# Own buffers for the token fetch, norm rows spread on TensorE, residual rows loaded earlier

## The chip, the cores and the metric

One core of a Trainium2 chip runs the whole program. The core has TensorE (matrix products and transposes), VectorE, ScalarE, GpSimd and the sync engine, which in this kernel only issues DMAs; 16 DMA engines move data between HBM and SBUF, the on-chip memory of 128 partitions. The metric is the time of one execution on the device in microseconds (us); lower is better.

## What is computed

One encoder layer: an attention mixer with a norm, then a mixture of experts with a second norm. Only the second part is touched. `x` has 512 tokens of 1024 channels.

```python
x = layer_norm(ALPHA * x + mixed, ln1_g, ln1_b)          # called h below
g_probs = softmax(x @ w_group + b_group)                 # best of 4 groups, then the best 2 of its 8 experts
combine = one_hot(group) * g_val * expert_w              # weight of each of 32 experts for each token
for g in range(4):                                       # 8 experts in each group, d_expert = 256
    hid = silu(einsum('nd,edf->nef', x, w_gate[g])) * einsum('nd,edf->nef', x, w_up[g])
    y = y + einsum('nef,efd->nd', hid * combine[:, g, :, None], w_down[g])
out = layer_norm(ALPHA * x + y, ln2_g, ln2_b)
```

## The kernel before

The attention part fills about the first 410 us and is left as it is. Then the experts follow, 0 to 31, in `trunk`'s last loop (lines 1278 to 1300). Tokens are gathered: each expert has 64 places, two experts make a pair, so a pair has a table column of 128 token numbers, `toki`, which `finish_routing` writes (line 920).

For expert `e` the loop calls `gate_up(e)` (16 matmul records in the trace, named sc<-we), `down(e - 1)` (8 records, tr<-we) and `act(e)` (four small transposes stp, then Silu). Every expert reads six weight tiles `we` of 128 x 1024 floats (0.5 MB each): four for gate and up, two for down; 192 in all. They are loaded by the sync queue in the order of use (`raw_load`, line 1018), up to `AHEAD` = 44 ahead of their use. The tiles' places are given by `RING` (line 67): a cycle of 40 entries, in which 0 is the pool `slots` (20 buffers), 1 is `slots2` (15 buffers), 2 and 3 are the pools `hip` and `lop` (4 each). The last 40 loads all go to `slots`. A load can be issued only when the tile that had its place has been used.

The first two pairs take their tokens from SBUF through products with one-hot matrices (`prep_first`). From pair 2 on, `fetch(p)` (line 1063) lets GpSimd gather 128 rows of h from HBM (`hD`) with an indirect DMA into a tile xg; there are `XGB` = 3 of these, taken from `slots2` when first needed and cleared by GpSimd. `prep_x` (line 1075) transposes such a tile on TensorE in two halves of four transposes each (pj<-ident,xg) and copies them to a tile xp. After the second expert of a pair, GpSimd scatters the pair's output rows oe to `y2D` in HBM (line 1147; oe has two buffers). The last two pairs, experts 28 to 31, stay in SBUF as tiles `late`.

Behind `act(28)` stand `gain_rows` (line 1181), which loads the two rows of the last norm (gain and bias) to one partition over ScalarE's DMA queue and spreads each over 128 partitions by two products with a row of ones, and `last_rows` (line 1157), which loads h again as four tiles hb and then y2D as eight tiles yy, both over the sync queue.

`finish` (line 1219) works off the list `FIN` step by step: `sum` adds two yy tiles on GpSimd, `open` begins the PSUM sum fin of one half of 128 tokens with hb times the identity, `add` adds the late rows by one-hot products, `rows` adds the yy sums, then the norm's statistics (`stat`, `root`, `gain`, `end`) and the stores follow.

Each engine works its own queue in order. Tile's scheduler sets the order of the instructions in the experts' part, and so may bring forward what is written later. The hardware-issued DMAs of the sync queue and of ScalarE share eight completion semaphores, named DMAHW0 to DMAHW7 below and handed out in turn; a DMA waits until the one before it on the same semaphore has landed.

Of the kernel before, what the change touches and what calls it, by code (L numbers as in the profile page):

```python
# [9 lines left out]
F32 = mybir.dt.float32  # L10
# [8 lines left out]
P = 128  # L19
S = 512  # L20
D = 1024
# [22 lines left out]
XEB = 4  # L44
AHEAD = 44
EARLY = 13
# [14 lines left out]
}  # L61
XGB = 3
H_POOL = (0, 1, 2, 3)
LATE_C = (2, 3)
H_STT = (0, 1, 2, 3)

RING = [0] * 8 + [1] * K2 + [0] * 12 + [2] * 4 + [3] * 4 + [1] * (NSLOT2 - XGB - K2)
SCB = 2
# [9 lines left out]
FIN_TAG = ("pj", "pj", "tr", "sc", "sc", "av", "tr", "tr")  # L78
FIN_AT = {}
FIN = (  # L80
# [17 lines left out]
def trunk(ctx, tc, xT, x, wm, wv, wbr, wout, wr, br, bg, rbx, lnp, lncol, wexp, out):  # L98
# [24 lines left out]
    def mm(ps, a, b, start, stop):  # L123
        pin(nc.tensor.matmul(ps, a, b, start=start, stop=stop))  # L124
# [23 lines left out]
    bgs = const.tile([P, 16], F32, name="bgs")  # L148
    lnc = const.tile([P, 2, C], F32, name="lnc")
    nc.gpsimd.dma_start(lnc, lncol)  # L150
# [4 lines left out]
    def slot(shape, dtype, name, pool=None):  # L155
        return (pool or slots).tile(shape, dtype, tag="slot", name=name)
# [535 lines left out]
    tok2 = keep.tile([P, 2 * NLATE], F32, name="tok2")  # L692
    flag = keep.tile([P, 1], I32, name="flag")
    onehot = keep.tile([P, TT, 4 * CAP], F32R, name="onehot")
    nc.gpsimd.memset(ones, 1.0)
# [364 lines left out]

    xg = []

    def fetch(p):
        if len(xg) < XGB:
            xg.append(slot([P, D], F32, f"xg{p}", slots2))
            nc.gpsimd.memset(xg[-1], 0.0)
        nc.gpsimd.indirect_dma_start(
            out=xg[(p - 2) % XGB], out_offset=None, in_=hD[:, :],
            in_offset=bass.IndirectOffsetOnAxis(ap=toki[:, p : p + 1], axis=0),
            bounds_check=S - 1, oob_is_err=False,  # L1070
        )
# [85 lines left out]
    def last_rows():  # L1157
# [12 lines left out]
        for tt in range(TT):  # L1170
            hb.append(slot([P, D], F32, f"hb{tt}", slots2))
            nc.sync.dma_start(hb[tt], hD[tt * P : (tt + 1) * P, :])
        for tt in range(TT):
            y2.append([slot([P, D], F32, f"yy{tt}{k}") for k in range(2)])
            for k in range(2):
                nc.sync.dma_start(y2[tt][k], y2v[tt, k])

    ones1 = bp.tile([1, P], F32, name="ones1")
    nc.gpsimd.memset(ones1, 1.0)

    def gain_rows():

        for k in range(2):
            gb2.append(lop.tile([P, D], F32, tag="lo", name=f"gb2{k}"))
            nc.scalar.dma_start(gb2[k][0:1, :], lnp[2 + k].unsqueeze(0))
            for j in range(2):
                ps = pb.tile([P, S], F32, tag="pj", name="pj", bufs=NBUF["pj"])
                mm(ps, ones1, gb2[k][0:1, j * S : j * S + S], True, True)
                nc.scalar.activation(gb2[k][:, j * S : j * S + S], ps, AF.Copy)
# [88 lines left out]
    for e in range(NE):  # L1278
# [12 lines left out]
        if 2 <= e < NE - 2:  # L1291
            prep_x(e // 2 + 1, e % 2)
            if e % 2 and e // 2 + 1 + XGB < NPAIR:
                fetch(e // 2 + 1 + XGB)
        if e == NE - 4:
            gain_rows()
            last_rows()
# [65 lines left out]
def layout(inputs):  # L1363
# [29 lines left out]
    lnp = np.stack([a["ln1_g"][0], a["ln1_b"][0], a["ln2_g"][0], a["ln2_b"][0]])  # L1393
    lncol = lnp[:2].reshape(2, C, P).transpose(2, 0, 1)
    gu = np.concatenate([a["w_gate"][0].reshape(NE, D, 256), a["w_up"][0].reshape(NE, D, 256)], 2)
# [23 lines left out]
```

## Time and profile before

| | us |
|---|---|
| median of 3 runs | 701.72 (699.74 to 704.83) |
| the profiled execution's own time | 704.91 |
| its span, first to last instruction | 703.2 |
| TensorE busy in the span | 651.9 (93%) |
| VectorE, ScalarE, GpSimd busy | 394.8, 322.8, 87.2 |
| moved by DMA | 160.15 MB, mean 228 GB/s |

A share of the span says little here: the attention part and the experts have different limits. So the stretch from 410 us on is read by itself: windows for who is busy, waits for who stands still, and the timeline for the order of events. A matmul's record is modelled and overlaps with the next one, so the pace is read from starts, not from the length of one record.

### The profile page before, as it was taken

The numbers are of one execution on the slowest core, as the hardware profiler recorded it, in microseconds if no ns is written. First come the engines' busy times: TensorE is split into PE (matmuls) and PEld (weight loads), VectorE is DVE, ScalarE is ACT, GpSimd is POOL, SyncE is SP. The second block draws the span as 40 slices with busy tenths as digits, with TensorE's granted clock in tenths as the row PEclk, the third lists the DMA queues.
The fourth block names the chain that finished last, engine by engine and source line by source line (L and its number), as shares of the span: only waits on it lengthen the run. The fifth ranks groups of instructions, "written<-read, shape, count | busy, mean of one in ns | idle before, by whom it ended". The sixth has DMA issues, their size and how long they took to land.

```text
span 703.2 us, 8791 instructions
## 1 busy us (share of the span) xinstructions
PE 651.9 (93%) x3072; PEld 425.1 (60%) x3072; DVE 394.8 (56%) x818; ACT 322.8 (46%) x632; POOL 87.2 (12%) x135
## 2 busy tenths in 40 slices
PE   8999998999999999999999979389999989999893
PEld 4888786888878878888888763133333333223251
DVE  5786868767777886464937973113323232322337
ACT  5777777866755666654422323112322222322312
POOL 2010100111000000040001330401111120100043
PEclk9999999999999999999999979889999999989997
DMA  9500095102130322138946689969999999499943
GB/s 335 234 1 1 1 348 220 62 6 86 46 105 23 113 76 89 61 114 301 334 192 223 226 334 409 410 248 412 408 409 411 406 404 404 161 365 410 410 191 122
DMA packets 48323, 160.15 MB, mean 228 GB/s; under 512 B 7440, under 2 KB 7584, under 8 KB 48276
## 3 DMA queue, kind: packets, MB, share of 16 engines
q1 hardware_dynamic: 44208, 152.26, 57.1%
q0 software_dynamic: 4064, 7.30, 2.8%
q8 instruction: 25, 0.41, 0.2%
q14 instruction: 22, 0.18, 0.1%
q10 hardware_dynamic: 4, 0.01, 0.0%
HBM read 151.20 MB, written 15.73 MB: 237 GB/s over the span
## 4 chain that ended last, share of the span: by engine, by line
PE 60%; issue 14%; DVE 12%; DMA 8%; ACT 3%; POOL 2%; SPq 0%; POOLq 0%; DVEq 0%
PE pj L124 23%; PE sc L124 9%; PE pv L124 6%; PE pb L124 6%; PE po L124 4%; DMA we<-in_wexp_dram 3%; PE tr L124 3%; PE av L124 2%; PE fin L124 2%; DMA xg<-hD,toki 2%; PE tr L521 2%; DMA hb<-hD 1%; DVE hp L804 1%; DVE gus L1106 1%; DMA y2D<-oe,rowi 1%
## 5 line engine op out<-in xcount | busy, mean ns | idle before, releaser
L124 PE MATMUL sc<-we,xp 128*64 128x512 f32 x448 | 117.6, 609 | 0.0
L124 PE MATMUL pj<-xh,wh 128*128 128x512 f32 x256 | 102.5, 402 | 2.6 <-DVE k L335 1.6
L124 PE MATMUL pj<-xh,wl 128*128 128x512 f32 x256 | 101.0, 394 | 0.5 <-DVE wl L109 0.5
L124 PE MATMUL pj<-xl,wh 128*128 128x512 f32 x256 | 100.8, 394 | 0.2 <-DVE xl L109 0.2
L124 PE MATMUL tr<-we,sg 128*64 128x512 f32 x256 | 78.6, 608 | 1.6 <-DVE sg L1119 1.6
L109 DVE TENSOR_TENSOR wl<-raw,wh 128x1024 fp32r<-128x1024 f32 (+1 forms) x57 | 68.4, 1205 | 20.4 <-ACT wh L106 20.1
L1106 DVE TENSOR_TENSOR gus<-gus,sc 64x512 f32<-64x512 f32 x32 | 21.7, 679 | 86.4 <-ACT gus L1105 86.3
L124 PEld LDWEIGHTS sc<-we,xp 128*64 128x64 f32 x448 | 33.0, 139 | 57.0 <-issue 53.5
L1105 ACT ACTIVATE gus<-sc 64x512 f32<-64x512 f32 x32 | 19.0, 593 | 105.4 <-PE sc L124 78.2
L106 ACT ACTIVATE wh<-raw 128x1024 fp32r<-128x1024 f32 (+1 forms) x57 | 58.7, 1038 | 16.9 <-PE pj L124 5.2
L124 PEld LDWEIGHTS pj<-xh,wh 128*128 128x128 f32 x256 | 48.4, 189 | 12.9 <-ACT wh L106 2.1
L124 PEld LDWEIGHTS pj<-xh,wl 128*128 128x128 f32 x256 | 48.3, 189 | 12.0 <-DVE wl L109 1.7
L124 PEld LDWEIGHTS pj<-xl,wh 128*128 128x128 f32 x256 | 48.5, 189 | 8.8 <-DVE xl L109 0.5
L124 PE MATMUL pb<-y,wh 128*128 128x512 f32 x128 | 39.9, 393 | 1.9 <-DVE k L335 1.9
L124 PEld LDWEIGHTS tr<-we,sg 128*64 128x64 f32 x256 | 21.1, 137 | 30.2 <-issue 26.6
L109 DVE TENSOR_TENSOR wl<-tr,wh 128x512 fp32r<-128x512 f32 (+1 forms) x64 | 30.8, 485 | 9.9 <-ACT wh L106 9.4
L1082 PE MATMUL pj<-ident,xg 128*128 128x128 f32 x112 | 19.6, 297 | 14.5 <-DMA xg<-hD,toki 14.5
L106 ACT ACTIVATE wh<-tr 128x512 fp32r<-128x512 f32 (+1 forms) x64 | 27.5, 431 | 12.1 <-PE tr L521 11.0
L474 POOL TENSOR_SCALAR_AFFINE_SELECT w<-w 128x128 f32<-128x128 f32 x32 | 14.5, 466 | 147.4 <-ACT w L471 144.7
L1147 POOL DMA_INDIRECT y2D<-oe,rowi x14 | 14.0, 1001 | 141.0 <-DVE oe L1145 141.0
L1082 PEld LDWEIGHTS pj<-ident,xg 128*128 128x128 f32 x112 | 12.5, 146 | 30.9 <-issue 13.7
L124 PE MATMUL sc<-k,q 128*128 128x512 f32 (+3 forms) x128 | 29.2, 324 | 0.9 <-DVE w L470 0.9
(222 smaller groups left out, 1205.4 us busy)
## 6 DMA issues: line engine op xcount, KB each, us to landing
we<-in_wexp_dram SPq DMA_DIRECT2D x192, 512.0 KB, 10.7
raw<-in_wm_dram SPq DMA_DIRECT2D x32, 512.0 KB, 4.9
raw<-in_wv_dram SPq DMA_DIRECT2D x8, 512.0 KB, 8.7
y2D<-zero SPq DMA_DIRECT2D x16, 256.0 KB, 3.9
raw<-in_wbr_dram SPq DMA_DIRECT2D x8, 512.0 KB, 5.5
raw<-in_wout_dram SPq DMA_DIRECT2D x8, 512.0 KB, 4.9
yy<-y2D SPq DMA_DIRECT2D x8, 512.0 KB, 10.2
strip<-in_rbx_dram SPq DMA_DIRECT2D x8, 256.0 KB, 4.2
```

Of the source, the lines that this page charges most:

```text
L106: act = nc.scalar.activation(hi, src, AF.Copy)
L109: pin((eng or nc.vector).tensor_sub(lo, src, hi.bitcast(F32)), fix == "both")
L124: pin(nc.tensor.matmul(ps, a, b, start=start, stop=stop))
L474: nc.gpsimd.affine_select(out=blk, in_=blk, pattern=[[-1, P]], compare_op=OP.is_gt, fill=0.0, base=0, channel_multiplier=1)
L521: nc.tensor.transpose(tr[:, i * P : (i + 1) * P], w[:, off + j * P : off + (j + 1) * P], ident)
L804: nc.vector.scalar_tensor_tensor(out=src, in0=src, scalar=r, in1=lnb[:, cs], op0=OP.mult, op1=OP.add)
L1082: nc.tensor.transpose(ps[:, c, :], xg[(p - 2) % XGB][:, o : o + P], ident)
L1105: nc.scalar.activation(gus[e], ps[CAP:], AF.Copy)
L1106: nc.vector.tensor_add(gus[e], gus[e], ps[:CAP])
L1147: nc.gpsimd.indirect_dma_start(out=y2D[:, :], out_offset=bass.IndirectOffsetOnAxis(ap=rowi[:, p : p + 1], axis=0), in_=oe[p], in_offset=No ...
```

## The change

The three fetch tiles xg get a place of their own (the pool `keep`) and are cleared when the tables for the routing are made. The three places in `slots2` go to weights: the ring has 43 entries, `AHEAD` is 47, and the last 43 loads go to `slots`. The norm's rows are no longer loaded to one partition: `lnc`, which already brought the first norm's rows as columns (channel on the partition), now brings all four, and for each of 16 blocks VectorE copies a column over 128 columns (bc, two buffers) and TensorE multiplies that with the identity. The loads of hb are written at expert 20 instead of 28, and the sums 0 to 3 are opened, and given the late rows that exist, from expert 29 on. The memory for GpSimd's DMA descriptors is set to 2048 bytes of a partition; the line gave no size before.

```diff
-AHEAD = 44
+AHEAD = 47
+HB_AT = 20
-RING = [0] * 8 + [1] * K2 + [0] * 12 + [2] * 4 + [3] * 4 + [1] * (NSLOT2 - XGB - K2)
+RING = [0] * 8 + [1] * K2 + [0] * 12 + [2] * 4 + [3] * 4 + [1] * (NSLOT2 - K2)
-FIN_AT = {}
+FIN_AT = {29: (0, 1, 2, 3)}
 FIN = (
-    "sum0 sum1 sum2 open0 open1 open2 open3 down31 open4 add4.2 add0.3 add1.3 add2.3 add3.3 add4.3 open5 add5.3 open6 add6.3 "
+    "sum0 sum1 sum2 down31 open4 add4.2 add0.3 add1.3 add2.3 add3.3 add4.3 open5 add5.3 open6 add6.3 "
...
-    lnc = const.tile([P, 2, C], F32, name="lnc")
+    lnc = const.tile([P, 4, C], F32, name="lnc")
...
+    xg = [keep.tile([P, D], F32, name=f"xg{k}") for k in range(XGB)]
+    for t in xg:
+        nc.gpsimd.memset(t, 0.0)
...
     def fetch(p):
-        if len(xg) < XGB:
-            xg.append(slot([P, D], F32, f"xg{p}", slots2))
-            nc.gpsimd.memset(xg[-1], 0.0)
...
         for tt in range(TT):
-            hb.append(slot([P, D], F32, f"hb{tt}", slots2))
-            nc.sync.dma_start(hb[tt], hD[tt * P : (tt + 1) * P, :])
-        for tt in range(TT):
             y2.append([slot([P, D], F32, f"yy{tt}{k}") for k in range(2)])
...
-    ones1 = bp.tile([1, P], F32, name="ones1")
-    nc.gpsimd.memset(ones1, 1.0)
...
             gb2.append(lop.tile([P, D], F32, tag="lo", name=f"gb2{k}"))
-            nc.scalar.dma_start(gb2[k][0:1, :], lnp[2 + k].unsqueeze(0))
             for j in range(2):
                 ps = pb.tile([P, S], F32, tag="pj", name="pj", bufs=NBUF["pj"])
-                mm(ps, ones1, gb2[k][0:1, j * S : j * S + S], True, True)
+                for q in range(4):
+                    c = 4 * j + q
+                    bc = bp.tile([P, P], F32, tag="bc", name="bc", bufs=2)
+                    nc.vector.tensor_copy(bc, lnc[:, 2 + k, c : c + 1].to_broadcast([P, P]))
+                    mm(ps[:, q * P : (q + 1) * P], bc, ident, q == 0, q == 3)
                 nc.scalar.activation(gb2[k][:, j * S : j * S + S], ps, AF.Copy)
...
+        if e == HB_AT:
+            for tt in range(TT):
+                hb.append(slot([P, D], F32, f"hb{tt}", slots2))
+                nc.sync.dma_start(hb[tt], hD[tt * P : (tt + 1) * P, :])
...
-    nc = bacc.Bacc("TRN2", target_bir_lowering=False, num_devices=1)
+    nc = bacc.Bacc("TRN2", target_bir_lowering=False, num_devices=1, dynamic_dma_scratch_size=2048)
```

How the instructions stand on the engines, at three places. A row is one instruction of the queue or several alike: its line, the operation, the tile written and the tiles read; the number behind a weight is its place among the 192, and the lines of the changed kernel are shifted.

The start of the fetches, on GpSimd before. y2D<-oe is a pair's scatter, xg2 to xg4 are the tiles for pairs 2 to 4.

```order
L947 TENSOR_TENSOR cw_3016<-cw_3016,small_oe_2972 128x32 x4
L1147 DMA y2D_60<-oe_4183,rowi_3017 1024x1024
L1147 DMA y2D_60<-oe_4287,rowi_3017 1024x1024
L1066 MEMSET xg2_4203 128x1024
L1066 MEMSET xg3_4208 128x1024
L1067 DMA xg2_4203<-hD_61,toki_3018 128x1024
L1067 DMA xg3_4208<-hD_61,toki_3018 128x1024
```

GpSimd at the same place now, where xg0 to xg2 are the tiles for pairs 2 to 4.

```order
L951 TENSOR_TENSOR cw_3016<-cw_3016,small_oe_2972 128x32 x4
L1066 DMA xg0_3024<-hD_61,toki_3018 128x1024
L1066 DMA xg1_3025<-hD_61,toki_3018 128x1024
L1066 DMA xg2_3026<-hD_61,toki_3018 128x1024
L1146 DMA y2D_60<-oe_4193,rowi_3017 1024x1024
L1066 DMA xg0_3024<-hD_61,toki_3018 128x1024
```

The three fetches stood behind the scatters of pairs 0 and 1; now they stand ahead of both.

TensorE before, from the end of gate_up(3) (weight 19) on to expert 3's down product and the first transposes (weights 20 and 21 are expert 2's down product, 26 and 27 expert 3's).

```order
L124 MATMUL sc_4267<-we19_4027,xe0_1_3989 64x512 x2
L124 MATMUL tr_4288<-we20_4029,sg_4257 64x512 x2
L124 MATMUL tr_4288<-we21_4031,sg_4257 64x512 x2
L1113 MATMUL stp_4299<-ident_63,gus_4284 128x64 x4
L124 MATMUL tr_4336<-we26_4041,sg_4304 64x512 x2
L124 MATMUL tr_4336<-we27_4043,sg_4304 64x512 x2
L1082 MATMUL pj_4261<-ident_63,xg2_4203 128x128 x4
L1082 MATMUL pj_4307<-ident_63,xg2_4203 128x128 x4
```

TensorE now, from the end of gate_up(2) on, whose last weight is 13.

```order
L125 MATMUL sc_4222<-we13_4019,xe0_1_3993 64x512 x2
L1081 MATMUL pj_4265<-ident_63,xg0_3024 128x128 x2
L125 MATMUL tr_4242<-we14_4021,sg_4210 64x512 x2
L125 MATMUL tr_4242<-we15_4023,sg_4210 64x512 x2
L1112 MATMUL stp_4256<-ident_63,gus_4239 128x64 x4
L1081 MATMUL pj_4265<-ident_63,xg0_3024 128x128 x2
L125 MATMUL sc_4271<-we16_4025,xe0_0_3980 64x512 x2
```

The first transposes stood behind all of expert 3; now they stand between gate_up(2) and gate_up(3), and expert 3's down product has moved behind gate_up(4)'s start.

The bunch of transposes on TensorE now, at expert 14 (xg0 holds pair 8 and at the end 11, xg1 pair 9, xg2 pair 10).

```order
L125 MATMUL sc_4761<-we79_4395,xp6_4656 64x512 x2
L1081 MATMUL pj_4801<-ident_63,xg2_3026 128x128 x2
L1081 MATMUL pj_4853<-ident_63,xg0_3024 128x128 x4
L125 MATMUL tr_4782<-we80_4419,sg_4751 64x512 x2
L1081 MATMUL pj_4899<-ident_63,xg0_3024 128x128 x2
...
L1081 MATMUL pj_4951<-ident_63,xg1_3025 128x128 x4
L125 MATMUL sc_4810<-we82_4427,xp7_4754 64x512 x2
...
L125 MATMUL sc_4810<-we84_4439,xp7_4754 64x512 x2
L1081 MATMUL pj_5095<-ident_63,xg2_3026 128x128 x4
L1081 MATMUL pj_5147<-ident_63,xg0_3024 128x128 x2
L125 MATMUL sc_4810<-we85_4443,xp7_4754 64x512 x2
```

TensorE before at the same expert: one half per expert, with pair 7's second half at the top and pair 8's first half below.

```order
L1082 MATMUL pj_4797<-ident_63,xg4_4213 128x128 x4
L124 MATMUL sc_4806<-we82_4439,xp7_4750 64x512 x2
L124 MATMUL sc_4806<-we83_4464,xp7_4750 64x512 x2
L124 MATMUL tr_4826<-we86_4476,sg_4794 64x512
L124 MATMUL sc_4806<-we84_4468,xp7_4750 64x512 x2
L124 MATMUL sc_4806<-we85_4472,xp7_4750 64x512 x2
L124 MATMUL tr_4826<-we86_4476,sg_4794 64x512
L124 MATMUL tr_4826<-we87_4485,sg_4794 64x512 x2
L1082 MATMUL pj_4849<-ident_63,xg2_4203 128x128 x4
```

A like bunch stood before at weights 108 to 118, with pairs 10 to 14; it has moved some four experts ahead. The norm rows' 16 products have moved from experts 25 and 26 to experts 21 to 23.

The sync queue before, with the semaphores that each load waits for, from weight 150 on.

```order
L1024 DMA we151_5011<-in_wexp_dram 128x1024 [waits DMAHW1_49,PE_49]
L1024 DMA we152_5015<-in_wexp_dram 128x1024 [waits DMAHW3_49,PE_49]
L1024 DMA we153_5023<-in_wexp_dram 128x1024 [waits DMAHW5_49,PE_49]
L1024 DMA we154_5027<-in_wexp_dram 128x1024 [waits DMAHW6_49,PE_49]
L1024 DMA we155_5052<-in_wexp_dram 128x1024 [waits DMAHW7_49,PE_49]
L1024 DMA we156_5056<-in_wexp_dram 128x1024 [waits DMAHW0_49,PE_49]
L1024 DMA we157_5060<-in_wexp_dram 128x1024 [waits DMAHW1_49,PE_49]
L1024 DMA we158_5064<-in_wexp_dram 128x1024 [waits DMAHW2_49,PE_49]
L1024 DMA we159_5073<-in_wexp_dram 128x1024 [waits DMAHW3_49,PE_49]
L1024 DMA we160_5077<-in_wexp_dram 128x1024 [waits DMAHW4_49,PE_49]
```

The sync queue now, at the new place of hb's loads.

```order
L1028 DMA we168_5125<-in_wexp_dram 128x1024 [waits DMAHW2_49,PE_49]
L1028 DMA we169_5129<-in_wexp_dram 128x1024 [waits DMAHW3_49,PE_49]
L1294 DMA hb0_5153<-hD_61 128x1024 [waits DMAHW4_49]
L1294 DMA hb1_5155<-hD_61 128x1024 [waits DMAHW5_49]
L1294 DMA hb2_5157<-hD_61 128x1024 [waits DMAHW6_49]
L1294 DMA hb3_5159<-hD_61 128x1024 [waits DMAHW7_49]
L1028 DMA we170_5162<-in_wexp_dram 128x1024 [waits DMAHW0_49,PE_49]
L1028 DMA we171_5166<-in_wexp_dram 128x1024 [waits DMAHW1_49,PE_49]
```

Before, the turn skips DMAHW2 ahead of weight 152 and DMAHW4 ahead of 153: ScalarE's two loads have them, so weights 158 and 160 wait for those. Now nothing is skipped, and hb's four loads have moved from behind weight 191 to behind 169; on TensorE the opens of sums 0 and 1 stand behind gate_up(28), those of 3 and 2 inside and behind gate_up(29).

## Rows read from the trace of the kernel before

**Rows 1.** Windows: start:end and length, busy time (instructions) of each engine, clock, DMA.

```profile
449.00:472.00 23.00, 11.63 (x52) 5.06 (x54) 2.23 (x4) 2.07 (x4) 7.82 (x8) 0.78 0.78 288
472.00:600.00 128.00, 123.89 (x596) 47.16 (x594) 38.58 (x66) 33.67 (x65) 18.97 (x19) 1.00 1.02 407
600.00:624.00 24.00, 22.90 (x88) 6.58 (x82) 7.36 (x17) 7.04 (x13) 1.19 (x2) 0.86 0.56 196
```

**Rows 2.** Timeline 426 to 463 us: start, length, engine, line, tiles, count [idle before].

```profile
430.62 0.17 DVE L920 TENSOR_SCALAR toki<-slotp 128x16 int32<-128x16 f32 x1 [0.50 <-PE slotp L124]
...
434.83 1.94 PE L124 MATMUL sc<-we,xe 128*64 128x512 f32 x8
...
446.12 1.94 PE L124 MATMUL tr<-we,sg 128*64 128x512 f32 x8 [1.56 <-DVE sg L1119]
...
450.82 1.86 POOL L1066 MEMSET xg<- 128x1024 f32 x2
452.85 1.04 POOL L1067 DMA_INDIRECT xg<-hD,toki  x1 [0.17 <-DMA we<-in_wexp_dram]
...
456.43 0.99 POOL L1067 DMA_INDIRECT xg<-hD,toki  x1 [0.27 <-POOL xg L1066]
...
460.37 1.97 PE L1082 MATMUL pj<-ident,xg 128*128 128x128 f32 x8 [12.31 <-DMA xg<-hD,toki]
```

**Rows 3.** Waits of the sync queue: us in total, times, longest.

```profile
SPq L1024 <- PE sc L124: 23.1, 23, 13.8
...
SPq L1024 <- DMA gb<-in_lnp_dram: 17.1, 2, 13.2
```

**Rows 4.** Timeline 608 to 634 us, the norm rows' loads and products.

```profile
610.11 1.92 ACTq L1185 DMA_DIRECT2D gb<-in_lnp_dram  x2
...
613.42 1.12 PE L124 MATMUL pj<-gb,ones 1*128 1x512 f32 x2
...
626.19 0.66 PE L1082 MATMUL pj<-ident,xg 128*128 128x128 f32 x4
```

**Rows 5.** The page's first line.

```profile
span 703.2 us, 8791 instructions
```

**Rows 6.** Timeline 660 to 684 us, the end of the experts and the opened sums.

```profile
661.20 1.08 PE L124 MATMUL tr<-we,sg 128*64 128x512 f32 x4
...
664.18 5.40 PE L124 MATMUL fin<-hb,ident 128*128 128x512 f32 x8 [1.90 <-DMA hb<-hD]
...
669.51 1.94 PE L124 MATMUL tr<-we,sg 128*64 128x512 f32 x8
670.73 2.36 POOL L1217 TENSOR_TENSOR yy<-yy,yy 128x1024 f32<-128x1024 f32 x1 [24.62 <-DMA yy<-y2D]
...
671.93 4.01 PE L124 MATMUL fin<-late,stl 128*128 128x512 f32 x15
...
679.35 1.88 PE L124 MATMUL fin<-yy,ident 128*128 128x512 f32 x4
```

**Rows 7.** The tile xg: its 14 fetches, from issue to landing.

```profile
DMA to landing us min/median/max: 4.8/7.4/8.4
```

**Rows 8.** Timeline of GpSimd, 470 to 600 us: three of the scatters, one per pair.

```profile
481.82 1.02 POOL L1147 DMA_INDIRECT y2D<-oe,rowi  x1 [5.88 <-DVE oe L1145]
...
549.82 1.00 POOL L1147 DMA_INDIRECT y2D<-oe,rowi  x1 [5.85 <-DVE oe L1145]
...
585.93 1.02 POOL L1147 DMA_INDIRECT y2D<-oe,rowi  x1 [16.56 <-DVE oe L1145]
```

**Rows 9.** Timeline of TensorE, 596 to 682 us: gate_up of experts 24, 25 and 28.

```profile
603.58 3.60 PE L124 MATMUL sc<-we,xp 128*64 128x512 f32 x16
...
609.89 3.60 PE L124 MATMUL sc<-we,xp 128*64 128x512 f32 x16
...
636.87 3.60 PE L124 MATMUL sc<-we,xp 128*64 128x512 f32 x16
```

**Rows 10.** Timeline of VectorE, 300 to 312 us: copies of a column over 128 columns.

```profile
306.71 0.53 DVE L670 COPY small_xe<-lnc 128x128 f32<-128x128 f32 x2
```

More of the change, by code (lines that the diff above doesn't have):

```diff
@@ L1058, in evac_x @@
             nc.vector.tensor_copy(dst, src)
-    xg = []
     def fetch(p):
-        if len(xg) < XGB:
-            xg.append(slot([P, D], F32, f"xg{p}", slots2))
-            nc.gpsimd.memset(xg[-1], 0.0)
         nc.gpsimd.indirect_dma_start(
@@ L1393, in layout @@
     lnp = np.stack([a["ln1_g"][0], a["ln1_b"][0], a["ln2_g"][0], a["ln2_b"][0]])
-    lncol = lnp[:2].reshape(2, C, P).transpose(2, 0, 1)
+    lncol = lnp.reshape(4, C, P).transpose(2, 0, 1)
     gu = np.concatenate([a["w_gate"][0].reshape(NE, D, 256), a["w_up"][0].reshape(NE, D, 256)], 2)
```

## The prediction

> **What bounds the kernel now.** I read the windows by stage first, because the change touches only what runs after 430 us. From 472 to 600 us the DMA engines move 407 GB/s at a share of 1.02 (full), and TensorE is busy 123.9 of 128 us [rows 1]: expert weights come as fast as they can and TensorE works them off, so a gain needs both. Then I looked for the places where one of the two stands still. There are two, and both are holes in the DMA stream as well.
>
> The first lies at 449 to 472 us: TensorE is busy 11.6 of 23 us, DMA share 0.78 [rows 1]. The timeline says why: the table of token numbers, toki, is ready at 430.8 us, but GpSimd issues the first fetch of token rows at 452.85, and TensorE's first transposes of them stand idle for 12.31 us until it lands [rows 2]. Meanwhile the weight buffers fill up and the sync queue waits 13.8 us in one piece for TensorE to free one [rows 3].
>
> The second is at 600 to 624 us: share 0.56 [rows 1]. TensorE is busy there, at a granted clock of 0.86 in the mean, so part of the time at 1.2 instead of 2.4 GHz; the stream stops because the sync queue's weight loads wait 17.1 us, 13.2 of it in one piece, for the two small loads of the last norm's rows [rows 3], which ScalarE issues only at 610.11 us, when its own queue gets there [rows 4]. The order shows the link: loads 158 and 160 wait for the channels DMAHW2 and DMAHW4 that those two took.
>
> Last I read the end. TensorE finishes expert 30's down product at 662.3 us, waits for hb, opens four sums in 5.40 us, runs down(31) until 671.45, and 31.75 us of sums, statistics and stores follow up to 703.2 [rows 5, 6].
>
> The sums are made against the profiled execution's span of 703.2 us. Its own time is 704.9 us, 3.2 above the median of the three runs (701.7); I take the difference in us over to the median.
>
> **The change, part by part.**
>
> *Fetch buffers of their own.* Nothing of the weight ring must come free, so the order puts the fetches of pairs 2, 3 and 4 ahead of all scatters. The first starts when toki is written, 430.9 us. Landings take 4.8 to 8.4 us, median 7.4 [rows 7]; with the stream full I take 7.4: 438.3 us. TensorE now has the first transposes behind gate_up(2), which ends at about 436.3 (the two records of load 16 taken off the end of the row at 434.83 [rows 2]). It waits 2.0 us (0 to 3.0), with expert 3's work queued behind. Gone are 12.31 us idle, 0.8 us because eight transposes, right behind the idle time and at the lower of the clock's two levels (mean 0.78 over the window [rows 1]), took 1.97 us instead of 2 x 0.6 [rows 2, 4], and 1.56 us ahead of down(3)'s products [rows 2], which now stand inside expert 4's. **Gain 12.31 + 0.8 + 1.56 - 2.0 = 12.6 us** (11.6 to 14.6).
> The three memsets (two take 1.86 us [rows 2], so 2.8 us of GpSimd) move to the end of the attention part, ahead of the index tables at 305 us that VectorE converts. I take 0: projections keep TensorE busy there. Without that cover it is 2.8 us.
>
> The Trainium skill (DMA: Bandwidth & Descriptors, section "Queues, rings and completion order") says that each DMA engine changes round-robin between the queues that have work, packet by packet. By that a fetch would pass the queued weights and land near the shortest of the rows, 4.8 us, before TensorE asks; TensorE's sum would be 2.0 us better. The median row, taken under a full stream, is 7.4 and speaks against it; the sum goes by the row.
>
> *The bunch of transposes.* Both orders pull several pairs' transposes together. Before, it lies at experts 18 and 19: two pairs of experts take 585.93 - 549.82 = 36.1 us where two others take 27.2 (five in 68.0 us) [rows 8]: 8.9 us more, of which eight halves brought forward are 8 x 0.6 = 4.7 [rows 4], paid back later, and some 4 are waits. Now it lies at experts 13 to 15. Pair 10's fetch can go out only behind pair 7's last transposes, and about 6.5 us of TensorE work stands between that and pair 10's transposes; a landing of 7.4 then leaves 1 us, pair 11 another. I take **0**; bounds -4 (no wait) and +12 (two more landings, little covered).
>
> *The norm rows.* Out: two loads and four one-row products. From expert 25 to 28 TensorE needs 636.87 - 609.89 = 26.98 us, against 3 x 6.31 without them [rows 9]: 8.05 us of products (1.1 each), their half clock and one half of transposes (0.6) [rows 4]. In: sixteen products of the transposes' shape at 0.15 each (2.4), around experts 21 to 23. Each waits for a copy on VectorE (two take 0.53 us [rows 10]) with two buffers; expert 22's matmuls stand between them, and behind the copies on VectorE stands that expert's gate sum. For these waits I take 1.5 us (0 to 8, every copy and product in turn). **Gain 8.05 - 0.6 - 2.4 - 1.5 = 3.5 us** (-3 to 5). And no load waits for a ScalarE channel any more.
>
> *hb and the opened sums.* Between down(30) and down(31) lie 7.2 us [rows 6]. About 0.4 remain for expert 31's gate. The four opens move to experts 28 and 29; at the full clock one takes 1.05 (two records, as the 1.1 of a product of that size [rows 4]), 4.2 in all. **Gain 2.6 us** (0 if they run slowly, 6.8 if they fall into waits for weights). Eight products of late rows also move ahead of down(31): 8 x 0.27 = 2.1 us [rows 6], no change in the sum. hb's four loads now run behind load 169, so the last weights come 5.2 us later than they would, and y2's rows are next behind them.
>
> **TensorE's sum:** 12.6 + 3.5 + 2.6 = **18.7 us**; down(31) ends at 671.45 - 18.7 + 2.1 = 654.9.
> **The stream's own limit:** filling the holes gives (1.02 - 0.78)/1.02 x 23 = 5.4 and (1.02 - 0.56)/1.02 x 24 = 10.8 us, 16.2 together [rows 1]. The first two y2 loads landed by 670.7 [rows 6], so now by 654.5; the last weight two loads of 1.29 us earlier (0.52 MB at 407 GB/s), 651.9. down(31) cannot end before 651.9 + 1.94 = 653.8. So TensorE sets the end by about 1 us: the two limits nearly meet, and a larger gain on TensorE alone is worth at most that.
> The tail then is 31.75 - 2.1 = 29.6 us. GpSimd's first sum of y2 ends at 654.5 + 2.4 = 656.9, before TensorE wants it (654.9 + 5.8 = 660.7), so it covers itself. End: 654.9 + 29.6 = 684.5, which is **683.0 us** on the median's scale.
>
> **Rivals.**
> *The first fetch passes the weights (7%).* Landing after 4.8 us, it ends TensorE's new wait; 2.0 us less there, but the stream's limit lets 1.0 through: 682. For it: the shortest landing [rows 7]. Against: the median. It is the skill's rule above.
> *A hole stays (10%).* The change does not do what it says for the stream: the sync queue meets another late thing, hb at load 170 or the last 43 loads, which have only 20 buffers. For it: TensorE ends only 1 us behind the stream, so any delay shows. Against: the holes' causes are gone from the order. With the second hole left, weights end at 662.7, down(31) at 664.6, the kernel at 694.2: 692.7.
> *The wait moves into the bunch (7%).* Two more landings uncovered at experts 13 to 15: +12 us, 695. For it: three buffers, four pairs in one and a half experts. Against: the same pattern cost some 4 us before.
> *GpSimd's transfers come one at a time (3%).* The smaller scratch lets GpSimd issue an indirect transfer only when the one before has landed. At 7.4 us each from 431, pair 9's fetch is the 13th (527 us), pair 10's the 15th (542), pair 11's the 16th (549); TensorE wants them from about 519 on (pair 5's scatter at 481.82 + 3 x 13.6 = 522.6, expert 14 six us later, less 12.6), and waits 8 + 13 + 5 us; pair 6's scatter lands at 579 and holds one of two output buffers, some 3 more. 683 + 29 = 712, slower. It decides between one and two in flight: with two, pair 9 lands by 480. Against: before, fetches started at 452.85 and 456.43 [rows 2], two at least in flight; the small scratch itself is in no trace here. The skill's page (same title, section "Terms") makes a descriptor 16 bytes, so 2048 would be 128 of them per ring; eight rows for each of 16 engines make that, as an estimate from the page, a dozen transfers.
>
> **How the numbers follow.** The forecast has 73%, the quicker first fetch 7, a hole that stays 10, the bunch 7, one at a time 3. Likeliest 683.0. TensorE's best case ends at the stream's limit, 681.9, and the runs of before spread 2.5 us each way; upward the range takes in the stayed hole. **678 to 693** leaves out about the bunch, the slow case and half of what the forecast's worst terms hold. 1% (7 us) is about what a measurement of this kernel tells from no change: faster 0.89, same 0.08, slower 0.03.
>
> **What would show it.** First fetch near 431 us; at most 3 us idle before the first transposes; no wait of weight loads on a ScalarE load; a DMA share of 1.0 from 449 on until the last y2 row; clock 1.0 at experts 25 to 28; down(31) ending near 655. The prediction is wrong if TensorE idles over 6 us in all at experts 13 to 15, if a later queue wait opens the stream again, or if weights land after 655 us although the stream was never idle.

## The result and the profile after

The changed kernel takes **695.33 us** (median of 4 runs, 693.07 to 695.99); the kernel before, run beside it, 702.34. The ratio is **0.9889** (95% interval 0.9862 to 0.9917). A second set of six runs gave 696.45 and 0.9915 (0.9887 to 0.9944). So the change is worth about 7 us of time where 18.7 were forecast, and 695.3 lies outside 678 to 693. The profiled execution's span is 694.3 us (its own time 695.99), 8.9 us under that of before [rows 5].

The windows of the changed kernel, with the columns of [rows 1]:

```profile
449.00:472.00 23.00, 23.00 (x114) 9.15 (x112) 7.51 (x14) 6.58 (x13) 3.79 (x4) 1.00 1.03 409
472.00:600.00 128.00, 121.06 (x590) 46.16 (x584) 41.07 (x84) 33.86 (x64) 17.32 (x18) 1.00 1.03 408
600.00:624.00 24.00, 22.04 (x110) 7.71 (x112) 6.47 (x12) 5.79 (x12) 1.94 (x2) 1.00 0.94 360
624.00:648.00 24.00, 21.85 (x92) 6.93 (x90) 5.91 (x10) 5.34 (x10) 0.98 (x1) 1.00 1.03 411
```

Both holes of the DMA stream are gone: share 1.03 for 0.78 in the first window, 0.94 for 0.56 in the third, and the granted clock is 1.00 at 600 to 624 us where it was 0.86. These are the signs that the prediction named. Yet TensorE gained less than half.

The timeline at the first fetch (start, length, engine, line, operation, tiles, count, idle before), which answers [rows 2]:

```profile
432.03 1.09 POOL L1066 DMA_INDIRECT xg<-hD,toki  x1 [14.50 <-DVE rowi L925]
433.43 1.00 POOL L1066 DMA_INDIRECT xg<-hD,toki  x1 [0.30 <-issue]
434.74 0.99 POOL L1066 DMA_INDIRECT xg<-hD,toki  x1 [0.31 <-issue]
439.51 0.44 PE L1081 MATMUL pj<-ident,xg 128*128 128x128 f32 x2 [1.80 <-DMA xg<-hD,toki]
```

Three fetches are issued within 2.7 us, the first lands after 7.4 us, and TensorE waits 1.80 us for it, not 12.31. That wait is the prediction's almost to the tenth. Behind it comes something that the prediction did not count. These are the products of down(1), and later those of down(2):

```profile
439.88 3.58 PE L125 MATMUL tr<-we,sg 128*64 128x512 f32 x8
...
447.64 1.89 PE L125 MATMUL tr<-we,sg 128*64 128x512 f32 x8
```

The same eight records take 1.7 us longer behind the wait: the granted clock is 0.57 at 440 to 444 us.

Where the rest went is read from one comparison: the start of the same gate_up in both kernels. First the kernel before, experts 9 and 20 (24 and 28 stand in [rows 9] as 603.58 and 636.87):

```profile
494.15 1.07 PE L124 MATMUL sc<-we,xp 128*64 128x512 f32 x2
...
577.60 1.08 PE L124 MATMUL sc<-we,xp 128*64 128x512 f32 x4
```

Then the changed kernel, experts 9, 20, 24 and 28, and the last twelve products of down(30) and down(31):

```profile
483.57 1.07 PE L125 MATMUL sc<-we,xp 128*64 128x512 f32 x2
...
568.25 1.51 PE L125 MATMUL sc<-we,xp 128*64 128x512 f32 x6
...
601.61 1.89 PE L125 MATMUL sc<-we,xp 128*64 128x512 f32 x8
...
626.85 1.46 PE L125 MATMUL sc<-we,xp 128*64 128x512 f32 x6
...
660.99 2.80 PE L125 MATMUL tr<-we,sg 128*64 128x512 f32 x12
```

TensorE's lead over the kernel before is the difference of these starts, and its steps can be set beside those of the prediction:

| up to | lead, us | step | the prediction's step |
|---|---|---|---|
| expert 9 | 10.6 | +10.6, first fetch | +12.6 |
| expert 20 | 9.35 | -1.2, bunch of transposes | 0 |
| expert 24 | 1.97 | -7.4, the norm's rows | -4.5 (2.4 + 1.5 + half 0.6) |
| expert 28 | 10.0 | +8.05, no one-row products | +8.05 |
| end of down(31), 671.45 and 663.8 | 7.7 | -2.4, opens and late rows | +0.5 (2.6 less 2.1 moved ahead) |
| end, 703.2 and 694.3 | 8.9 | +1.2, tail | +2.1 |

No single wait took the gain. Four steps came out smaller than forecast, all on the same side, 8.9 us up to down(31). A second trace of the changed kernel agrees in the two largest: 33.36 us from expert 20 to 24 in both, 36.94 from expert 28 to the end of down(31) for 36.93 here.

The bunch of transposes, with TensorE's waits for fetches and the uncut sixteen records of a gate_up behind it, in the changed kernel:

```profile
524.32 0.63 PE L1081 MATMUL pj<-ident,xg 128*128 128x128 f32 x4 [0.69 <-DMA xg<-hD,toki]
...
528.03 0.41 PE L1081 MATMUL pj<-ident,xg 128*128 128x128 f32 x2 [1.48 <-DMA xg<-hD,toki]
...
532.49 3.60 PE L125 MATMUL sc<-we,xp 128*64 128x512 f32 x16
535.92 1.03 PE L125 MATMUL tr<-we,sg 128*64 128x512 f32 x4
537.60 0.46 PE L1112 MATMUL stp<-ident,gus 64*128 64x64 f32 x4 [0.65 <-DVE gus L1105]
```

And the wait in the bunch of the kernel before:

```profile
570.26 0.41 PE L1082 MATMUL pj<-ident,xg 128*128 128x128 f32 x2 [2.15 <-DMA xg<-hD,toki]
```

The norm's rows, experts 21 to 22, in the changed kernel's timeline:

```profile
581.70 1.29 PE L125 MATMUL pj<-ident,bc 128*128 128x128 f32 x6
582.93 1.08 PE L125 MATMUL sc<-we,xp 128*64 128x512 f32 x4
583.94 0.49 PE L125 MATMUL pj<-ident,bc 128*128 128x128 f32 x2
584.35 1.08 PE L125 MATMUL sc<-we,xp 128*64 128x512 f32 x4
585.36 1.30 PE L125 MATMUL pj<-ident,bc 128*128 128x128 f32 x6
```

and the group of all of them, from the lines of TensorE at 560 to 600 us (records, busy us, mean ns, idle before):

```profile
L125 PE MATMUL pj<-ident,bc 128*128 128x128 f32 x32 | 6.5, 310 | 0.3
```

There are 32 records, not 16: a product of two f32 tiles leaves two records where a transpose leaves one. TensorE hardly idles there (0.3 us); it works. And a group of four gate_up products that is cut off from the next by other products takes 1.01 us from start to start (582.93 to 583.94), against 0.86 in the uncut sixteen above (532.49 to 535.92, 3.43 for four groups). So each cut costs 0.15 us here.

The end of the experts, the counterpart of [rows 6]: expert 31's gate_up with late rows between, and the opens that are left.

```profile
652.35 1.03 PE L125 MATMUL sc<-we,xp 128*64 128x512 f32 x4
654.08 0.73 PE L125 MATMUL fin<-late,stl 128*128 128x512 f32 x2 [0.70 <-DVE late L113]
654.74 1.07 PE L125 MATMUL sc<-we,xp 128*64 128x512 f32 x2
655.75 0.73 PE L125 MATMUL fin<-late,stl 128*128 128x512 f32 x2
```

The same stands in expert 30. TensorE waits 0.70 us each time for VectorE to write the late rows, with the rest of gate_up queued behind.

### The profile page after: what moved, and what is told of

The parts are those of the page before. It is cut to its first block, busy times and chain, and to the rows that moved or that the text cites. A ratio compares the mean times of both kernels' runs of the same rounds, so it can differ in the third digit from the quotient of the medians.

```text
span 694.3 us, 8852 instructions
## 1 busy us (share of the span) xinstructions
PE 652.4 (94%) x3096; PEld 425.1 (61%) x3096; DVE 399.3 (58%) x834; ACT 323.2 (47%) x632; POOL 86.9 (13%) x134
## 4 chain that ended last, share of the span: by engine, by line
PE 59%; DVE 16%; issue 14%; ACT 6%; DMA 3%; POOL 2%; SPq 0%; POOLq 0%; DVEq 0%; ACTq 0%
PE pj L125 19%; PE sc L125 12%; PE pv L125 6%; PE pb L125 6%; PE po L125 4%; PE tr L125 3%; PE av L125 2%; PE fin L125 2%; DVE gus L1105 2%; PE tr L522 1%; DVE wl L110 1%; ACT wh L107 1%; PE stp L1112 1%; DVE hp L808 1%; DMA y2D<-oe,rowi 1%
## 5 line engine op out<-in xcount | busy, mean ns | idle before, releaser
L125 PE MATMUL sc<-we,xp 128*64 128x512 f32 x448 | 115.2, 600 | 0.0
L125 PE MATMUL tr<-we,sg 128*64 128x512 f32 x256 | 76.5, 616 | 0.0
L125 PEld LDWEIGHTS tr<-we,sg 128*64 128x64 f32 x256 | 19.7, 137 | 26.9 <-issue 22.5
L1112 PEld LDWEIGHTS stp<-ident,gus 64*128 64x128 f32 x128 | 10.3, 138 | 36.1 <-DVE gus L1105 28.7
L125 PEld LDWEIGHTS pb<-y,wh 128*128 128x128 f32 x128 | 23.3, 188 | 7.1 <-PE tr L522 1.7
```

The lines of the kernel that those rows point to most:

```text
L1112: nc.tensor.transpose(st[:, q, :], gus[e][:, q * P : (q + 1) * P], ident[:CAP, :CAP])
```

## The experiments

Two theories were set against each other. **W**: TensorE's own work sets the end everywhere, and the terms for that work were too small. **S** (later L, and H for a hole in it): the weight stream sets the end, so that what TensorE gains is lost again where weights are late. Spans of one kernel differ by some 2 us for a reason that no edit here touches: the experts' first matmul starts between 419.2 and 422.5 us over all profiled executions, and the granted clock of 411 to 449 us lies between 0.84 and 0.96. So within a trace I read the distance between two experts, not the absolute time.

### Each part alone

**The fetch buffers alone.** The kernel before with

```diff
-AHEAD = 44
+AHEAD = 47
-RING = [0] * 8 + [1] * K2 + [0] * 12 + [2] * 4 + [3] * 4 + [1] * (NSLOT2 - XGB - K2)
+RING = [0] * 8 + [1] * K2 + [0] * 12 + [2] * 4 + [3] * 4 + [1] * (NSLOT2 - K2)
+    xg = [keep.tile([P, D], F32, name=f"xg{k}") for k in range(XGB)]
...
+    nc = bacc.Bacc("TRN2", target_bir_lowering=False, num_devices=1, dynamic_dma_scratch_size=2048)
```

> The kernel before, with the first part of the change alone: three fetch tiles of their own, their three places given to weights, the small descriptor memory; norm rows and hb as before. Theory W (TensorE's own work sets the end everywhere): in the changed kernel TensorE stood 10.6 us ahead of before at expert 9 and 9.4 us at expert 20, so this part alone is worth 9.4 us and gives a ratio of 0.987 (0.984 to 0.990): more than the whole change measured (0.9889). Theory S (the weight stream sets the end): the hole for the norm's two loads is still there, only 5.4 us of stream are filled; ratio 0.992. First fetch lands near 439 us and TensorE waits 1.8 us for it in both.

Measured: 701.00 us, ratio 0.995 (0.9927 to 0.9973), span 699.6. That is neither: TensorE's lead was 11.6 us at expert 9 and 10.3 at expert 28, as W says, but only 3.6 at the end. Windows of this kernel, its sync queue's wait for the norm's loads, and TensorE's end of the experts:

```profile
520.00:560.00 40.00, 35.62 (x180) 13.20 (x178) 11.51 (x20) 9.79 (x19) 6.68 (x7) 1.00 0.82 314
560.00:600.00 40.00, 37.64 (x154) 11.80 (x150) 12.71 (x25) 11.24 (x21) 2.95 (x3) 0.91 0.88 338
```

```profile
SPq L1027 <- DMA gb<-in_lnp_dram: 18.8, 2, 16.6
```

```profile
642.42 1.08 PE L124 MATMUL sc<-we,xp 128*64 128x512 f32 x4 [0.49 <-DMA we<-in_wexp_dram]
643.87 1.08 PE L124 MATMUL sc<-we,xp 128*64 128x512 f32 x4 [0.37 <-DMA we<-in_wexp_dram]
...
654.11 1.08 PE L124 MATMUL sc<-we,xp 128*64 128x512 f32 x4 [0.20 <-DMA we<-in_wexp_dram]
655.47 1.08 PE L124 MATMUL tr<-we,sg 128*64 128x512 f32 x4 [0.28 <-DMA we<-in_wexp_dram]
...
660.54 5.40 PE L124 MATMUL fin<-hb,ident 128*128 128x512 f32 x8 [2.47 <-DMA hb<-hD]
```

The hole has moved with the work to 520 to 600 us and is worth (1.02 - 0.82)/1.02 x 40 + (1.02 - 0.88)/1.02 x 40 = 13.3 us of stream. TensorE does not wait for weights there, for there are enough in the buffers. It is paid 80 us later: from 642 on each group of four products waits for its weight tile, and then TensorE waits for hb.

**The norm's rows alone.** The kernel before with the new `gain_rows`, `lnc` of four rows, and the small descriptor memory.

> The kernel before, with the norm's rows spread on TensorE from columns as in the change, and the small descriptor memory to make room; fetch tiles and hb as before. Theory W: 32 records and the broken overlap around them cost some 7.4 us, against some 8 us of the four one-row products with their slow clock: 0.7 us gained, and up to 1.9 us more because hb no longer comes late; ratio 0.996 to 0.999. Theory S: the hole of the stream at 600 to 612 us is filled, 10.8 us; weights and hb land earlier by that and the time falls by 5 us or more, ratio under 0.993.

Measured: 702.01 us, ratio 0.9975 (0.9954 to 0.9995): W's range.

**hb and the opens alone.** The kernel before with

```diff
-FIN_AT = {}
+FIN_AT = {29: (0, 1, 2, 3)}
-    "sum0 sum1 sum2 open0 open1 open2 open3 down31 open4 ...
+    "sum0 sum1 sum2 down31 open4 ...
+        if e == HB_AT:
+            for tt in range(TT):
+                hb.append(slot([P, D], F32, f"hb{tt}", slots2))
+                nc.sync.dma_start(hb[tt], hD[tt * P : (tt + 1) * P, :])
```

> The kernel before, with hb loaded at expert 20 and the sums 0 to 3 opened from expert 29 on as in the change; fetch tiles and norm rows as before. Theory W: from expert 28 to down(31) the changed kernel lost 2.4 us of TensorE's lead by this and got 1.2 back behind down(31), so this part alone makes the kernel slower by 1 us, ratio 1.000 to 1.003. My prediction's step: 2.6 us gained, 0.996.

Measured: 705.21 us, ratio 1.0028 (0.9999 to 1.0057). In its trace expert 28 starts at 637.16 (0.3 behind the kernel before), down(31) ends 2.6 us behind, the kernel 1.2 us behind. The gain of 2.6 us is not there; the trace has some 1 us lost, and the interval reaches from no change to a loss of 4 us. TensorE waits 0.70 us for a late row here too:

```profile
655.60 0.73 PE L125 MATMUL fin<-late,stl 128*128 128x512 f32 x2 [0.70 <-DVE late L113]
```

The three parts alone give -0.5%, -0.25% and +0.3%, together about half of what the whole gives. They are not additive: the fetch part needs a stream without the hole, as the next kernel shows.

### The hole by itself

The kernel with the fetch buffers alone, once more, with one word changed, so that GpSimd's queue issues the norm's two small loads. TensorE and the sync queue keep their order.

```diff
-            nc.scalar.dma_start(gb2[k][0:1, :], lnp[2 + k].unsqueeze(0))
+            nc.gpsimd.dma_start(gb2[k][0:1, :], lnp[2 + k].unsqueeze(0))
```

> The kernel with the fetch buffers alone, in which the two small loads of the norm's rows are issued by GpSimd's queue instead of ScalarE's; the order of TensorE and of the sync queue is the same, row for row. Theory H (the fetch part's gain was lost in the hole that the sync queue's wait of 16.6 us for those loads leaves): the hole goes, TensorE keeps its 10 us of lead to the end and does not wait for hb; ratio 0.983 to 0.987 where the fetch part alone gave 0.995. Rival (TensorE's one-row products or the late hb took the gain): 0.993 to 0.996 again.

Measured: 689.37 us, ratio **0.9813** (0.9777 to 0.9849), span 687.8. That is a little better than theory H's range and far from the rival's. The windows that were open, and the opens that waited 2.47 us for hb:

```profile
520.00:560.00 40.00, 35.63 (x180) 13.34 (x180) 11.29 (x20) 9.56 (x18) 6.09 (x7) 1.00 1.02 403
560.00:600.00 40.00, 37.60 (x166) 12.30 (x164) 12.58 (x26) 11.89 (x22) 4.13 (x5) 0.96 1.02 407
```

```profile
650.30 3.70 PE L124 MATMUL fin<-hb,ident 128*128 128x512 f32 x8 [0.53 <-DMA hb<-hD]
```

The lead of 12.5 us at expert 28 is carried to the end of down(31); it is 15.6 us there, because the kernel before waits 1.90 us for hb and opens the sums in 5.40 us [rows 6]. So the wait of the sync queue for a load that another engine issues late cost the fetch part 1.4% of the time, some 10 us, and by the ratios this kernel, without the change's other two parts, is 5 to 7 us faster than the changed one.

**The same word in the kernel before.**

> The kernel before with the same edit alone: the two small loads issued by GpSimd's queue. Theory H: the hole at 600 to 612 us goes, but TensorE has no lead that could use it; only its 1.9 us of waiting for hb and a part of the half clock behind the hole are to be had: ratio 0.995 to 0.998. Theory S (the stream sets the end already in before): 5 to 10 us, 0.985 to 0.993.

Measured: 714.93 us, ratio 1.0171 (1.014 to 1.0201): slower, which no theory had. In this order the two loads stand on GpSimd behind the scatter at 616.67 us, which waits for an expert's output; TensorE comes to the products first:

```profile
624.09 2.07 PE L124 MATMUL pj<-gb,ones 1*128 1x512 f32 x2 [5.79 <-DMA gb<-in_lnp_dram]
```

```profile
624.00:648.00 24.00, 23.46 (x52) 5.77 (x54) 2.60 (x5) 4.22 (x8) 0.00 (x0) 0.55 0.43 140
```

It waits 5.79 us, and then it works through 24 us at a granted clock of 0.55, nearly all at the lower level of 1.2 GHz. So the edit is no test of the hole in the kernel before; it put a wait in the hole's place.

### The terms of TensorE's work

**Transposes for products.** The changed kernel with

```diff
-                    mm(ps[:, q * P : (q + 1) * P], bc, ident, q == 0, q == 3)
+                    nc.tensor.transpose(ps[:, q * P : (q + 1) * P], bc, ident)
```

> The changed kernel, in which the sixteen blocks of the norm's rows are spread by TensorE transposes of the copied column instead of products with the identity; the copies on VectorE and their two buffers stay. Theory W: a transpose leaves one record where a product leaves two; 16 records of some 0.16 us instead of 32 of some 0.19, so from expert 21 to 24 TensorE gives back 3 to 4 us less, ratio to before 0.984. Rival V (the copies on VectorE and their two buffers set the pace there): no faster than the changed kernel, 0.989, and idle time of TensorE before the transposes.

Measured: 694.07 us, ratio 0.9876 (0.9828 to 0.9923), span 689.9. The ratio does not tell it from the changed kernel; the trace does. From expert 20 (565.79) to expert 24 (597.24) it takes 31.45 us, where the changed kernel takes 33.36: 1.9 less, where theory W had 3 to 4. Both theories were right in part, for now some copies come late:

```profile
579.25 0.44 PE L1184 MATMUL pj<-ident,bc 128*128 128x128 f32 x2
579.89 0.47 PE L1184 MATMUL pj<-ident,bc 128*128 128x128 f32 x2 [0.21 <-DVE bc L1183]
```

**No products at all.** The changed kernel with the rows loaded to all partitions.

```diff
-            for j in range(2):
...
-                nc.scalar.activation(gb2[k][:, j * S : j * S + S], ps, AF.Copy)
+            nc.sync.dma_start(gb2[k], lnp[2 + k].partition_broadcast(P))
```

> The changed kernel, in which the norm's two rows are loaded to all 128 partitions by two broadcast loads of the sync queue; no products, no copies. Theory W (TensorE's work alone): its 5.9 us of products and some 1.5 us of broken overlap around them go, span 687, ratio 0.979. Theory L (the stream is the next limit): the two loads bring 1 MB more, 2.6 us at 407 GB/s; last weight near 656, down(31) not before 658, where it ended at 663.8 in the changed kernel; span 689, ratio 0.981 to 0.983. If the norm rows were not what TensorE lost its lead by, no change, 0.989.

Measured: 689.82 us, ratio **0.9823** (0.9805 to 0.984), span 686.0. Expert 20 starts at 564.89, expert 24 at 591.70: 26.8 us, 6.6 less than in the changed kernel. So the spreading cost 6.6 us, where 3.9 had been put down. And now TensorE has caught up with the stream. Each group that waits has the wait in brackets; the last two rows are the late products that stand before the last weight's, and these:

```profile
646.46 1.08 PE L125 MATMUL sc<-we,xp 128*64 128x512 f32 x4 [0.20 <-DMA we<-in_wexp_dram]
647.83 1.08 PE L125 MATMUL tr<-we,sg 128*64 128x512 f32 x4 [0.29 <-DMA we<-in_wexp_dram]
...
652.93 2.11 PE L125 MATMUL fin<-late,stl 128*128 128x512 f32 x8 [0.28 <-DVE stl L1165]
654.97 1.07 PE L125 MATMUL tr<-we,sg 128*64 128x512 f32 x2
```

The last weight landed at 651.5 us; the prediction's limit of the stream was 651.9. The ratio is in theory L's range, but L's landing (656) and its end of down(31) (not before 658; it was 656.0) are not: the two broadcast loads are issued from 642.60 us on, behind the last weight, and so delay no weight.

**The masks ahead.** The kernel just shown, with the masks stl of the late rows written ahead of the broadcast loads, so that they don't stand before the last product.

> The changed kernel with the norm's rows by two broadcast loads of the sync queue, and the masks of the late rows written ahead of these loads, so that VectorE makes them before expert 29 and not between the last matmuls. With the broadcast loads alone, down(31) had its last weight at 651.5 us but ended at 656.0, behind 2.2 us of mask making on VectorE and eight late products. Theory L (the stream sets the end): down(31) ends at 653.5 to 654.5, ratio 0.979 to 0.982 where the loads alone gave 0.982. If TensorE is the limit there: the same or slower, since eight late products move ahead.

Measured: 688.78 us, ratio **0.979** (0.9763 to 0.9817), span 687.5. Its interval overlaps that of the kernel without this edit, so the two are not told apart. In the profiled execution down(31) ended at 657.1, not at 654: TensorE began the experts 1.2 us later, ran a slower clock ahead of expert 5, and came to expert 28 3.2 us behind, and from 638 us on it waits for no weight, so it was TensorE and not the stream that set the end there. From expert 20 to 24 it again took 26.8 us (568.09 to 594.89).

**The opens back at their old place.** The changed kernel, hb still loaded at expert 20, with

```diff
-FIN_AT = {29: (0, 1, 2, 3)}
+FIN_AT = {}
-    "sum0 sum1 sum2 down31 open4 ...
+    "sum0 sum1 sum2 open0 open1 open2 open3 down31 open4 ...
```

> The changed kernel with hb still loaded at expert 20, but the sums 0 to 3 opened where before opened them, between down(30) and down(31), and no late rows ahead of down(31). Theory W: opens cost 4.3 us wherever they stand; TensorE's two waits of 0.7 us for late rows between experts 30 and 31 go and some work moves behind down(31): 1 us faster than the changed kernel, 0.987. My prediction's step (the early opens themselves save): 1 to 3 us slower, 0.991 to 0.993.

Beside it ran the changed kernel:

> The changed kernel once more, beside the others of this call: ratio 0.987 to 0.991. TensorE's start on the experts and its slow clock ahead of expert 5 differ by one to two us from run to run (419.3 to 421.3 us so far), so the span is read against those.

Measured: 692.60 us, ratio 0.9863 (0.9845 to 0.9881), against 0.9915 (0.9887 to 0.9944) beside it, which is just above what was expected. The late place is the faster of these two; the changed kernel's first ratio, 0.9889 (0.9862 to 0.9917), would not tell them apart. In the traces, expert 28 starts at 624.20 and down(31) ends 33.5 us later, against 36.9 in the changed kernel; the tail takes back 1.3, so 2.1 us are won. And here too TensorE meets the stream:

```profile
649.41 1.08 PE L125 MATMUL tr<-we,sg 128*64 128x512 f32 x4 [0.27 <-DMA we<-in_wexp_dram]
...
653.00 2.84 PE L125 MATMUL fin<-hb,ident 128*128 128x512 f32 x6
```

**Both: transposes and the old place.**

> The changed kernel with both edits: transposes for the norm's rows and the late place of the opens. Theory W: 2.1 us by the records, 0.3 by the overlap and 1 us by the opens, ratio 0.984. Theory L: the last weight lands at 653.7 us as it did with the transposes alone, down(31) not before 655.6, so all of this still comes through.

Measured: 693.42 us, ratio 0.9863 (0.984 to 0.9886): no better than the old place alone, against both theories' 2.4 us more. In its trace TensorE gains 1.9 us from expert 20 to 28 on the kernel above, by the transposes; but down(30) waits for its weight in both (at 651.4 us here, at 649.4 above, and the experts started 2.6 us later here), so what the transposes had won is waited away there, and the opens come behind that wait.

**Broadcast loads and the old place.**

> The changed kernel with the norm's rows by broadcast loads and the late place of the opens (between down(30) and down(31)). Theory L: the early opens cost nothing when TensorE waits for weights from expert 30 on, so moving them behind adds 4.3 us behind down(30); 1 to 2 us slower than with the loads alone, 0.984 to 0.986. Theory W: as in the changed kernel, the late place is the faster by 1 to 3 us, 0.979 to 0.981.

Measured: 690.65 us, ratio 0.9821 (0.9793 to 0.9849), the same as the broadcast loads with the early opens (0.9823), and between the two theories. Where TensorE waits for the stream, the place of the opens decides nothing that these runs can tell.

## Why the prediction was wrong

**What held.** The holes, their causes and their going; the first fetch (432.03 for 431, landing after 7.4 us, a wait of 1.80 for 2.0); no wait of weight loads for ScalarE; the clock at experts 25 to 28; and the stream's own limit, which the kernel with broadcast loads reaches within 0.4 us. That kernel's span of 686.0 is near the 684.5 that was forecast for the change, but that is luck: it spends nothing on the norm's rows, for which the forecast had 3.9 us. The three memsets cost nothing that shows, as forecast: the experts start at 419.2 to 422.5 us in the kernels with them, at 419.6 to 421.3 in those without. The skill's rule of turns between queues (the Trainium skill, DMA: Bandwidth & Descriptors, "Queues, rings and completion order"), by which the prediction's rival let the fetch land after some 4.8 us, did not show here: it landed at the old median, 7.4.

**The step that failed** is the sum of TensorE's work, with its sentence "TensorE sets the end by about 1 us: the two limits nearly meet". TensorE ended 8.9 us later than forecast (663.8 for 654.9), so that the stream had time to spare. By terms:

- *Norm rows, "sixteen products of the transposes' shape at 0.15 each (2.4)"*: 2.9 us. The shape was the same, the operation was not. A product of f32 tiles leaves two records, and the rows ahead of the prediction said so: one-row products and opens were counted there with two records each, transposes with one. From start to start the 32 records take 6.2 us, most of the 6.6 that the broadcast loads gave back; the cuts in gate_up are in the rest. With transposes it is 4.6, near the 3.9 forecast. The wait for copies (1.5 allowed) was hardly there with the products (0.3 us); with the quicker transposes some of it appeared. The Trainium skill (FP8 and Floating Point Precision, "TensorE Precision Notes") has a true f32 product pass the array four times. The trace agrees in so far as the product costs more than the transpose, and shows two records.
- *hb and the opened sums, "Gain 2.6 us"*: 2.9 us. The gap of 7.2 us did close. But 4.2 us of opens, 2.6 of late rows (2.1 forecast), two waits of 0.70 for these rows and some 1 us of cuts in gate_up took its place. The waits were not in the sum: the late rows of expert 28 and 29 are added as soon as they are written, so TensorE's queue stands still until VectorE has written them. With the opens back at their old place 2.1 us of this came back.
- *First fetch*: 2.0 us. 0.9 of it is the start of the experts (420.6 for 419.6), which varies that much from run to run; with that added back the step is 11.5, just under the bound of 11.6. The rest is the clock: the 1.7 us that down(1) lost behind the wait of 1.80 us, for which the sum had no term. That too varies: of ten traces with the fetch buffers three have it, with 35.8 to 36.0 us from the experts' start to expert 5, and the other seven take 34.0 to 34.5.
- *Bunch*: 1.2 us, inside its bounds. TensorE waits for fetches as long as before (0.7 and 1.5 us, 2.15 before). But before the bunch gate_up and down alternate so that the small transposes never wait, and behind it each expert waits 0.55 to 0.65 us for VectorE's gate sum: a pair takes 13.6 us ahead of the bunch and 14.04 behind it (532.49 to 546.53). The bunch now comes five experts sooner, and two and a half more pairs in the second way make 1.1 us. This is read from the traces alone; no run moved the bunch.
- *Tail*: 0.9 us more than forecast; what took it stays open.

**The scale.** The forecast took 3.2 us off the profiled time because the three runs shown had a median of 701.7. With 4 to 25 runs, medians of before were 702.3, 702.8, 703.8 and 704.2. The changed kernel's profiled execution stood 0.7 above its median. So some 2.5 of the 12.3 us by which the time was missed are the scale.

**The rivals.** None of them came. One at a time on GpSimd is out (three fetches in flight at 435 us). "A hole stays" has the right mechanism in the wrong kernel: with the fetch part alone it happens, and costs some 10 us (0.995 to 0.9813).

## What to carry to other kernels

Count the records of an operation, not its shape: an f32 product and a transpose of the same tiles are two different prices, and here each cut that other products made in a run of gate_up cost 0.15 us more. Where the queues of two engines share completion semaphores, one engine's late load becomes the other's hole, and such a hole is paid when the buffers run dry, here 80 us later; so look for it in the share of the stream, not among the waits of the engine beside it. And a small forecast that is the sum of several terms misses by the sum of their errors when these all fall to one side: let the terms' lower bounds make the range together, not one by one.

## What the runs showed that was not expected

TensorE's granted clock can fall without an idle engine. In the kernel before TensorE is busy 22.9 of 24 us at 600 to 624 us and has a clock of 0.86 [rows 1]; around the one-row products of the two kernels with the fetch buffers alone it is 0.91 and 0.96 at 560 to 600 us, where the changed kernel, without these products, has 1.00. In the kernel before with GpSimd's loads it fell in an idle time of 5.79 us and then stayed at 0.55 for 24 us, with TensorE busy 23.46 of them, while the four one-row products were worked off between groups of gate_up and down. What these stretches have in common is products with a single row of operands; no run here separates that from other causes. Nor is it the only way to a lower clock: the kernel with the norm's rows alone, without such products, also has 0.96 at 560 to 600 us, there behind a wait of 2.10 us for a fetch, while the kernel before waits 2.15 us at the like place and keeps 1.00.

GpSimd's queue took two small loads without holding up the sync queue (its waits for gb, 18.8 us, are gone), but its own order then decides when they start: 562.6 us behind the ninth scatter in one kernel, 617.6 us behind the twelfth in the other, 55 us apart.
